# Linear attention on one core: the last pair's Q load cut into unequal software DMAs, the last store in two whole ones

## The chip, the core and the metric

The kernel runs on one core of a Trainium2 chip. The time is device microseconds of one execution, the median of the runs on the chip. An execution with the hardware profiler on gives the page and the trace; its own time stands beside its span below.

## The reference

`Q`, `K` and `V` are float32 arrays of 8 batches, 12 heads, 512 positions and 64 features, 12.58 MB each. Per batch and head:

```python
Q_feat = np.maximum(0, Q) + 1
K_feat = np.maximum(0, K) + 1
KV = np.einsum('bhkd,bhkv->bhdv', K_feat, V)
K_sum = np.sum(K_feat, axis=2)
numerator = np.einsum('bhqd,bhdv->bhqv', Q_feat, KV)
denominator = np.einsum('bhqd,bhd->bhq', Q_feat, K_sum)
return (numerator / (denominator[:, :, :, None] + 1e-10)).astype(np.float32)
```

The output is float32, another 12.58 MB. Every input is read once and the output written once.

## The kernel before, in words

The 96 heads are worked on in twelve groups of eight, two groups to a pair, so there are six pairs (`s` = 0 to 5, groups `2*s` and `2*s + 1`). A pair's load of one input is 2 MB: 128 partitions, and per partition two runs (`n`) of 32 rows of 64 values, 8 KB of float32 each. The loads are issued from GpSimd (POOL) as software DMAs, since they convert float32 to bfloat16 on the way into SBUF; only the very first half of Q comes through SyncE (SP) as float32. `load_pair(s)` issues V, K and Q of a pair in this order (L111, L111, L124). In the first pair each input comes in halves.

For each group VectorE makes the features of K and Q (`feature`, L154), and VectorE and ScalarE together spread V into four masked blocks (`v_blocks`, L171 and L173). TensorE multiplies features of K with the blocks of V (`keys_values`, L195); a column of ones in the blocks gives the sum of K's features in the same product. ScalarE copies the result to SBUF (L209). Q's features are transposed on TensorE (L222) and copied by ScalarE (L227). `out_matmuls` (L237) makes numerators and denominators, and `norms` on VectorE takes the reciprocal (L253) and the product (L254) into `o_sb`, the pair's output tile in SBUF.

The order is written out by hand (`manual_schedule`): `iteration(s)` works on the keys of pair `s` while the outputs of pair `s - 1` are finished; each engine runs its instructions in the order of the program and waits on semaphores. `load_pair(s + 2)` is issued after iteration `s`, and the load of the last pair (s = 5) after iteration 3. The stores of the first six groups are held back until then, so that POOL issues them behind all loads; the stores of groups 6 and 7 follow iteration 4 and those of groups 8 and 9 iteration 5. Each of these ten is one software DMA of 1 MB (L138). The software DMAs take their completion semaphores from a ring of eight, in the order of issue.

The last two groups are stored through SP (hardware DMAs). Group 10 is one DMA of 1 MB (L143). Group 11 is cut: pairs of heads 1 and 5 in one DMA of 512 KB (L146), 3 in one of 256 KB (L147), and 7 in three: the last two of its eight rows per partition (512 bytes) in one DMA of 123 partitions and one of 5 (L150), and the first six rows in one of 128 (L151).

A DMA's data moves through sixteen DMA engines that all queues share. The trace records a completion step of each engine for each DMA, and each packet's queue, start, duration and size, but not the engine that moved it.

Of the kernel before, what the change touches and what calls it, by code (L numbers as in the profile page):

```python
# [19 lines left out]
def kernel(  # L20
# [15 lines left out]
    nc = tc.nc  # L36

    B, H, S, D = Q.shape
    P = 128
    C = 8  # L40
# [4 lines left out]
    NP = 4  # L45
    NG = NPAIR // NP
# [4 lines left out]
    def view(t, c):  # L51
        return t.flatten_outer_dims().rearrange("(n p c) d -> p n c d", p=P, c=c)

    q_eights = view(Q, C4)
# [30 lines left out]
    outs = {}  # L85
# [35 lines left out]

    def load_q(s):
        t = in_pool.tile([P, 2, C4, D], BF16, name="q_raw")
        nc.gpsimd.dma_start(out=t, in_=q_eights[:, 2 * s : 2 * s + 2])  # L124
        rows = t.rearrange("p n (r c) d -> p n r c d", c=C)
        for e in range(2):
            raw["q", 2 * s + e] = [rows[:, n, :, 4 * e : 4 * e + 4] for n in range(2)]

    def load_pair(s):
        load("v", (2 * s, 2 * s + 1))  # L130
        load("k", (2 * s, 2 * s + 1))
        load_q(s)

    def store(g):
        s = g // 2
        o_to = o_dram[:, 2 * NP * s : 2 * NP * s + 2 * NP]
        if g < NG - 2:
            nc.gpsimd.dma_start(  # L138
                out=o_to[:, g % 2 : 2 * NP : 2], in_=outs[s][:, g % 2 : 2 * NP : 2], single_packet=True
            )  # L140
            return
        if g == NG - 2:
            nc.sync.dma_start(out=o_to[:, 0 : 2 * NP : 2], in_=outs[s][:, 0 : 2 * NP : 2])  # L143
            return
        o_sb = outs[s]
        nc.sync.dma_start(out=o_to[:, 1 : 2 * NP : NP], in_=o_sb[:, 1 : 2 * NP : NP])  # L146
        nc.sync.dma_start(out=o_to[:, 3], in_=o_sb[:, 3])  # L147
        cut = C - 2
        for ps in (slice(0, 123), slice(123, P)):
            nc.sync.dma_start(out=o_to[ps, 7, cut:], in_=o_sb[ps, 7, cut:])  # L150
        nc.sync.dma_start(out=o_to[:, 7, 0:cut], in_=o_sb[:, 7, 0:cut])  # L151

    def feature(dst, src):
        nc.vector.tensor_scalar(  # L154
# [167 lines left out]
    with tc.manual_schedule():  # L322
# [8 lines left out]
            out=mask,  # L331
            in_=identity.rearrange("p (h b x) -> p b h x", h=2, b=4),
# [3 lines left out]
        for i in range(2):  # L336
            t = v_all[:, i].rearrange("p n c b x -> p (n c) b x")
            nc.vector.memset(t[:, :, :, D1:], 0.0)
            nc.vector.tensor_copy(  # L339
                out=t[:, :, :, D], in_=mask[:, None, :].to_broadcast([P, 2 * C2, 4])  # L340
# [18 lines left out]
        for s in range(1, NG // 2):  # L359
            iteration(s)  # L360
            if s + 2 < NG // 2:
                load_pair(s + 2)
            for g in range(2 * s - 2, 2 * s) if s > 3 else range(2 * s) if s == 3 else ():
                store(g)
        output(NG - 2)
        output(NG - 1)
        for g in range(NG - 2, NG):
            store(g)
# [30 lines left out]
```

## Time and profile before

| | |
|---|---|
| median of 3 runs | 126.42 us (126.39 to 126.56) |
| profiled execution, its own time | 126.47 us |
| its span, first to last instruction | 124.7 us |
| TensorE busy | 72.2 us (58%) |
| VectorE busy | 81.9 us (66%) |
| ScalarE busy | 68.4 us (55%) |
| GpSimd busy, DMA issues included | 24.8 us (20%) |
| HBM read and written | 37.75 MB and 12.58 MB, 404 GB/s over the span |
| software DMA queue | 7520 packets, 28.84 MB, 93.9% of the DMA engines' time |
| hardware DMA queue | 1368 packets, 3.15 MB, 6.8% |

A load's packets are counted by what they write, which is half of what they read, since the type is halved on the way; a store's packets are counted in full. In the row of slices each digit is a fortieth of the span. "POOLq" and "SPq" are the two issuing queues. The time from a DMA's issue to its landing holds the time that it waited behind other DMAs in the queue.

### The profile page before, as it was taken

To read this page: it belongs to the slowest core of one execution; us is meant where nothing else is said; L and a number is where in the kernel's file an instruction comes from. 1 tells how busy PE (TensorE), PEld (TensorE's weight loads), DVE (VectorE), ACT (ScalarE), POOL (GpSimd) and SP (SyncE) were. 2 spreads that over 40 slices of the span, in tenths; PEclk is the share of its full clock that TensorE was granted. 3 is DMA by queue.
4 is the path that set the end of the run, shared out by engine and by line. 5 is a ranking of instruction groups with operands and counts; after the bars stand their busy time and mean duration, and the time that the engine had idled before them with its cause. 6 is when DMAs were issued, how large, how long until landed. Compare 5 with 4: busy or idle time off the path is not lost.

```text
span 124.7 us, 3086 instructions
## 1 busy us (share of the span) xinstructions
PE 72.2 (58%) x1344; PEld 54.4 (44%) x1344; DVE 81.9 (66%) x185; ACT 68.4 (55%) x73; POOL 24.8 (20%) x52
## 2 busy tenths in 40 slices
PE   0000199692397949976796927979429995550000
PEld 0000299591266725754465714567216774320000
DVE  0475643006679997999979979798997945990000
ACT  0005827928955999199947998059990196000000
POOL 6990001500000600033000890220210202000000
PEclk9999999999859995899769995599975799955555
DMA  3999999999999999999999999999999999999991
GB/s 74 344 216 217 214 212 210 214 214 222 210 212 210 218 222 212 212 212 214 221 214 213 212 216 216 218 213 210 214 350 422 413 417 413 413 413 418 411 388 64
DMA packets 8902, 32.18 MB, mean 258 GB/s; under 512 B 568, under 2 KB 824, under 8 KB 8760
## 3 DMA queue, kind: packets, MB, share of 16 engines
q0 software_dynamic: 7520, 28.84, 93.9%
q1 hardware_dynamic: 1368, 3.15, 6.8%
q8 instruction: 10, 0.16, 0.5%
q14 instruction: 4, 0.03, 0.1%
HBM read 37.75 MB, written 12.58 MB: 404 GB/s over the span
## 4 chain that ended last, share of the span: by engine, by line
PE 32%; DMA 21%; ACT 18%; DVE 14%; issue 3%; POOL 1%; ACTq 0%; POOLq 0%
PE kva_ps L195 21%; DMA k_raw<-in_K_dram 14%; ACT qt L227 9%; PE o_ps L237 7%; DMA v_raw<-in_V_dram 7%; ACT v_all L173 6%; DVE o_sb L254 6%; DVE v_all L171 4%; PE qt_ps L222 4%; ACT kva_all L209 2%; DVE kf L154 2%; DVE recip L253 1%; ACT L173 1%; POOL v_raw L111 1%; POOL k_raw L114 1%
## 5 line engine op out<-in xcount | busy, mean ns | idle before, releaser
L195 PE MATMUL kva_ps<-v_all,kf 64*64 64x272 bf16 x768 | 41.0, 330 | 19.9 <-ACT v_all L173 18.3
L195 PEld LDWEIGHTS <-kf 64*64 64x64 bf16 x768 | 28.3, 125 | 25.7 <-DVE v_all L171 16.4
L173 ACT ACTIVATE v_all<-v_raw,mask 128x1024 bf16<-128x1024 bf16 (+1 forms) x24 | 36.5, 1578 | 3.1 <-DMA v_raw<-in_V_dram 3.0
L254 DVE TENSOR_TENSOR o_sb<-o_ps,recip 128x512 f32<-128x512 f32 x48 | 33.2, 691 | 1.7
L227 ACT COPY qt<-qt_ps 128x1024 bf16<-128x1024 bf16 x24 | 22.7, 1024 | 19.6 <-PE qt_ps L222 19.6
L237 PE MATMUL o_ps<-kva_all,qt 128*64 128x130 bf16 x384 | 21.4, 253 | 14.1 <-ACT kva_all L209 9.2
L237 PEld LDWEIGHTS <-qt 128*64 128x64 bf16 x384 | 14.9, 126 | 23.8 <-issue 9.6
L171 DVE TENSOR_SCALAR v_all<-v_raw,mask 128x2048 bf16<-128x2048 bf16 (+1 forms) x36 | 22.0, 665 | 3.2 <-DMA v_raw<-in_V_dram 3.2
L154 DVE TENSOR_SCALAR kf<-k_raw 128x1024 bf16<-128x1024 bf16 x24 | 9.4, 434 | 12.0 <-DMA k_raw<-in_K_dram 12.0
L222 PE MATMUL qt_ps<-identity,qf 128*128 128x128 bf16 x192 | 13.7, 219 | 4.9 <-ACT qt L227 4.8
L253 DVE RECIPROCAL recip<-o_ps 128x8 f32<-128x8 f32 x48 | 9.6, 201 | 8.3 <-PE o_ps L237 8.2
L111 POOL DMA_DIRECT2D v_raw<-in_V_dram x5 | 3.7, 730 | 53.5 <-ACT qt L227 23.7
L222 PEld LDWEIGHTS <-qf 128*128 128x128 bf16 x192 | 11.2, 97 | 7.0 <-issue 6.4
L138 POOL DMA_DIRECT2D out_dram<-o_sb x10 | 8.1, 819 | 25.5 <-DVE o_sb L254 13.7
L209 ACT CAST kva_all<-kva_ps 64x260 bf16<-64x260 f32 x24 | 9.0, 374 | 3.8 <-PE kva_ps L195 3.5
L154 DVE TENSOR_SCALAR qf<-q_raw 128x1024 bf16<-128x1024 bf16 x22 | 8.2, 430 | 0.1
L173 ACT ACT_TABLE_LOAD x1 | 1.3, 1283 | 10.7 <-DMA v_raw<-in_V_dram 10.7
L124 POOL DMA_DIRECT2D q_raw<-in_Q_dram x5 | 3.6, 722 | 0.0
L111 POOL DMA_DIRECT2D k_raw<-in_K_dram x5 | 3.6, 719 | 0.0
L330 DVE TENSOR_REDUCE mask<-identity 128x4 f32<-128x128 bf16 x1 | 0.3, 285 | 4.7 <-POOL identity masks.py:199 4.7
L344 POOL MEMSET kva_all<- 128x130 bf16 x16 | 2.4, 204 | 0.0
L339 DVE CAST v_all<-mask 128x128 bf16<-128x128 f32 x2 | 2.2, 1644 | 0.0
(11 smaller groups left out, 6.0 us busy)
## 6 DMA issues: line engine op xcount, KB each, us to landing
out_dram<-o_sb POOLq DMA_DIRECT2D x10, 1024.0 KB, 24.6
v_raw<-in_V_dram POOLq DMA_DIRECT2D x5, 1024.0 KB, 13.5
k_raw<-in_K_dram POOLq DMA_DIRECT2D x5, 1024.0 KB, 17.7
q_raw<-in_Q_dram POOLq DMA_DIRECT2D x5, 1024.0 KB, 21.9
o_sb<-in_Q_dram SPq DMA_DIRECT2D x1, 1024.0 KB, 5.0
k_raw<-in_K_dram POOLq DMA_DIRECT2D x2, 512.0 KB, 9.7
v_raw<-in_V_dram POOLq DMA_DIRECT2D x2, 512.0 KB, 11.6
out_dram<-o_sb SPq DMA_DIRECT2D x1, 1024.0 KB, 11.5
```

Of the source, the lines that this page charges most:

```text
L111: nc.gpsimd.dma_start(out=t, in_=drams[x][:, 2 * s : 2 * s + 2])
L138: nc.gpsimd.dma_start(out=o_to[:, g % 2 : 2 * NP : 2], in_=outs[s][:, g % 2 : 2 * NP : 2], single_packet=True)
L154: nc.vector.tensor_scalar(out=dst, in0=src, scalar1=1.0, scalar2=1.0, op0=ALU.add, op1=ALU.max)
L171: nc.vector.tensor_scalar_mul(block[:, 0:cut], v_raw[:, 0:cut], mask[:, b : b + 1])
L173: nc.scalar.mul(out=block[:, cut:], in_=v_raw[:, cut:], mul=mask[:, b : b + 1])
L195: nc.tensor.matmul(halves[h][64 * eight : 64 * eight + 64, 0 : 4 * DV], lhsT=kf[ps, c, n, :], rhs=v_all[ps, g % 2, n, c], start=first, sto ...
L209: nc.scalar.copy(out=kva[ps, :, n, :], in_=halves[h][ps, 0 : 4 * DV].rearrange("p (b x) -> p b x", b=4)[:, :, 0:D1],)
L222: nc.tensor.transpose(qt_ps[g][half][:, c, r], qf[:, r, 2 * half + c, :, :], identity)
L227: nc.scalar.copy(out=qts[g // 2][:, lo : lo + 2], in_=t.rearrange("p c r q -> p c q r"))
L237: nc.tensor.matmul(o_ps[64 * j : 64 * j + 64, c // 2 % 2, (c % 2) * W : (c % 2) * W + W], lhsT=qt[:, c, q : q + 16, :], rhs=kva[:, b], sta ...
L253: nc.vector.reciprocal(out=recip, in_=cells[:, :, :, :, D:D1])
L254: nc.vector.tensor_tensor(out=outs[g // 2][:, 2 * h + g % 2 : 2 * NP : NP, 4 * i : 4 * i + 4].rearrange("p n (b c) d -> p b c n d", b=2), ...
```

## The change

The Q load of the last pair (s = 5) becomes six software DMAs. The first four of the 32 rows, for both runs `n`, are loaded by five DMAs over 51, 4, 51, 5 and 17 partitions, which together are the 128; then the other 28 rows are loaded by one DMA over all 128 partitions. The values and where they are put in `q_raw` stay the same, and so do the other pairs.

The last group's store becomes two hardware DMAs of 512 KB over all 128 partitions: pairs of heads 1 and 5, as before, and 3 and 7.

```diff
     def load_q(s):
         t = in_pool.tile([P, 2, C4, D], BF16, name="q_raw")
-        nc.gpsimd.dma_start(out=t, in_=q_eights[:, 2 * s : 2 * s + 2])
+        q_from = q_eights[:, 2 * s : 2 * s + 2]
+        cut = 0
+        if s == NG // 2 - 1:
+
+            cut = 4
+            lo = 0
+            for n in (51, 4, 51, 5, 17):
+                ps = slice(lo, lo + n)
+                nc.gpsimd.dma_start(out=t[ps, :, 0:cut], in_=q_from[ps, :, 0:cut])
+                lo += n
+        nc.gpsimd.dma_start(out=t[:, :, cut:], in_=q_from[:, :, cut:])
         rows = t.rearrange("p n (r c) d -> p n r c d", c=C)
...
         if g == NG - 2:
             nc.sync.dma_start(out=o_to[:, 0 : 2 * NP : 2], in_=outs[s][:, 0 : 2 * NP : 2])
             return
-        o_sb = outs[s]
-        nc.sync.dma_start(out=o_to[:, 1 : 2 * NP : NP], in_=o_sb[:, 1 : 2 * NP : NP])
-        nc.sync.dma_start(out=o_to[:, 3], in_=o_sb[:, 3])
-        cut = C - 2
-        for ps in (slice(0, 123), slice(123, P)):
-            nc.sync.dma_start(out=o_to[ps, 7, cut:], in_=o_sb[ps, 7, cut:])
-        nc.sync.dma_start(out=o_to[:, 7, 0:cut], in_=o_sb[:, 7, 0:cut])
+        nc.sync.dma_start(out=o_to[:, 1 : 2 * NP : NP], in_=outs[s][:, 1 : 2 * NP : NP])
+        nc.sync.dma_start(out=o_to[:, 3 : 2 * NP : NP], in_=outs[s][:, 3 : 2 * NP : NP])
```

## The prediction

> **What bounds the kernel now.** I read the page first: it has no compute engine above 66%, but the DMA row is full from the second slice on.
>
> ```profile
> PE 72.2 (58%) x1344; PEld 54.4 (44%) x1344; DVE 81.9 (66%) x185; ACT 68.4 (55%) x73; POOL 24.8 (20%) x52
> ...
> DMA  3999999999999999999999999999999999999991
> GB/s 74 344 216 217 214 212 210 214 214 222 210 212 210 218 222 212 212 212 214 221 214 213 212 216 216 218 213 210 214 350 422 413 417 413 413 413 418 411 388 64
> ```
>
> The loads count at half their size here (float32 read, bfloat16 written: 215 GB/s written is 430 read), the stores at full size. So the transfers run at one rate all along, and the end is the end of the DMA queues. The timeline of the last stretch agrees: VectorE's last product ends at 112.05 us, and SyncE has nothing left to issue after 117.9.
>
> ```profile
> 111.36 0.69 DVE L254 TENSOR_TENSOR o_sb<-o_ps,recip 128x512 f32<-128x512 f32 x1
> 112.08 0.34 SPq L147 DMA_DIRECT2D out_dram<-o_sb  x1
> 112.46 4.28 SPq L150 DMA_DIRECT2D out_dram<-o_sb  x2
> 116.78 1.11 SPq L151 DMA_DIRECT2D out_dram<-o_sb  x1
> ```
>
> The table by stretches says how it runs out: full to 121, a third busy after.
>
> ```profile
> 118.00:121.00 3.00, 0.00 (x0) 0.00 (x0) 0.00 (x0) 0.00 (x0) 0.00 (x0) 0.50 1.04 405
> 121.00:124.00 3.00, 0.00 (x0) 0.00 (x0) 0.00 (x0) 0.00 (x0) 0.00 (x0) 0.50 0.34 125
> ```
>
> Who is still busy then? The trace keeps, for each DMA, sixteen completion steps, one per DMA engine, without the engine's name. For the DMA landed at 97.50 us eight engines finish at 96.14 to 96.69 and eight at 97.26 to 97.50. For the one landed at 111.33, seven finish by 109.22, seven by 110.04, two at 111.27 and 111.33. For the very last store, fourteen finish between 121.31 and 122.58 and two at 123.70 and 123.75. So two late engines set the end, 1.1 us behind the next. Their lateness has a visible cause: the page's queues hold instruction loads beside the data.
>
> ```profile
> q8 instruction: 10, 0.16, 0.5%
> q14 instruction: 4, 0.03, 0.1%
> ```
>
> Each of the ten 16 KB packets took 0.89 to 1.03 us of one engine, and after each of them one engine's completions step back by 1.1 to 1.2 us. The first eight hit eight different engines; the ninth (97.41 us) and tenth (105.27) hit two of these again, and these are the two late ones. The 8 KB packets (0.31 us; 44.6, 72.7, 102.3 and 116.65 us) put one or two of the other eight behind as well. When compute ends there are seven leaders and nine laggards, among them the two last.
>
> **What the change moves, part by part.** Prices of packets: hardware stores of 512 B took 27 ns, of 1,536 B 65, of 2,048 B 84, so about 8 ns a packet and 0.037 ns a byte. A 2 MB load occupies each engine 4.89 us (landings 87.55 to 92.45) for 128 KB: 26.8 GB/s.
>
> (1) The last store. Per engine, pairs 3 and 7 are now eight 2,048 B and eight 1,536 B packets: 0.67 + 0.52 = 1.19 us, and three engines also get 41 packets of 512 B (1.1 us). That it is three shows in the trace: the 123-partition store has three completions from data, the 5-partition one five. After it, every engine has sixteen packets of 2,048 B, 1.34 us, and one completion step less: +0.14 us on the two late engines, which is on the path. Three SyncE issues (4.28 + 1.11 us) become less than 0.4 us; they hide behind the queue's backlog now (last issue 117.9, data moving to 123.7), so that is worth nothing.
>
> (2) The main Q load shrinks from 8 KB to 7 KB a row on 16 rows per engine: 16 KB at 26.8 GB/s, -0.61 us on every engine.
>
> (3) The 256 KB taken out come back in pieces of 1 KB read. I take how a count of partitions is dealt out from the stores: 123 went to 3 engines, 5 to 5, 128 to 16, in each the largest divisor up to 16. Then 51 goes to 3 engines (17 partitions each), 4 to 4, 5 to 5, 17 to 1 engine. Together 3 + 4 + 3 + 5 + 1 = 16: if each begins where the last ended, seven engines carry 17 partitions and nine carry 1. No row shows software DMAs of this size, so I bound a 1 KB piece: 38 ns at the bulk rate, 46 by the packet prices. Two pieces a partition: 34 pieces cost 1.29 to 1.56 us, two cost 0.08 to 0.09. Completion steps: 9 ns (hardware) to 22 ns (software median) each, one to five more per engine: 0.01 to 0.11. Net with (2): a light engine gets -0.53 to -0.41, a heavy one +0.69 to +1.06. I take -0.43 and +1.0, near the dear end, since small packets were dear in the store.
>
> The rule for these shares is also in the Trainium skill, "DMA: Bandwidth & Descriptors", section "Why a DMA increments its semaphore by 16 and not by 1": largest common divisor up to 16, software DMAs on consecutive engines from a cursor that goes round. The store's three and five completions agree with the divisor; no run here shows the cursor. The same section notes an exception, software copies dealt out over all sixteen; that is the second rival.
>
> (4) POOL's queue. The five added issues cost some 0.55 to 0.72 us each, and POOL is 80% idle. More matters who they wait for. Software DMAs use eight semaphores in turn, and each waits for the one eight before it. The waits show it, and POOL's timeline its first case: the store at 78.04 came 0.3 us after the Q load of eight DMAs earlier landed (77.76).
>
> ```profile
> POOL out_dram L138 <- DMA v_raw<-in_V_dram: 4.4, 1, 4.4
> ...
> POOL out_dram L138 <- DMA q_raw<-in_Q_dram: 3.2, 1, 3.2
> ```
>
> ```profile
> 70.58 0.72 POOL L124 DMA_DIRECT2D q_raw<-in_Q_dram  x1
> 71.29 3.51 POOL L138 DMA_DIRECT2D out_dram<-o_sb  x4
> 78.04 0.75 POOL L138 DMA_DIRECT2D out_dram<-o_sb  x1 [3.24 <-DMA q_raw<-in_Q_dram]
> 83.22 0.85 POOL L138 DMA_DIRECT2D out_dram<-o_sb  x1 [4.42 <-DMA v_raw<-in_V_dram]
> ```
>
> With five more in the ring, the fifth small load waits for the K load that landed at 72.87, and the main Q load takes the place of the store at 78.04; behind it on POOL stand all ten stores. The first then waits for the V load (82.67), the second for the K load (87.55), the next five only for small loads that have landed, so by 93 us eight stores are issued, as before. Cover: at 78.7 the queue still holds V until 82.67, K until 87.55 and the small pieces; the first store, issued near 83.5, is wanted at about 92. Cost nothing; without that cover each microsecond of an empty queue is a microsecond of time.
>
> (5) Q's landing. Light engines end it near 92.0, heavy ones that lead now (91.1 to 91.6) near 92.6; VectorE reads Q at 96.84. Four microseconds of room, so nothing; nor do the extra semaphore waits on VectorE, which has 8 us of backlog behind it.
>
> **Sum.** If both late engines are light: -0.43 + 0.14 = -0.29 us. The profiled execution took 126.47 with a span of 124.7, 1.8 us around it; the median of the runs is 126.42. 126.42 - 0.29 = 126.13. Next in line: leaders finished pair 3 at 120.65 to 121.15; with a whole pair 7 (0.65) and a heavy share they end by 122.9, before 123.46. A middle engine (pair 3 done by 122.03) with a heavy share ends at 123.4 to 123.7, just level with the late ones. So 126.03 to 126.40 in this case.
>
> Why light? The three engines of the 123-partition store must be leaders: a middle one (121.74) with 1.1 + 0.52 us more would end at 123.4, and none ends between 122.58 and 123.70. The two further engines of the 5-partition store end among the middle ones. So a first heavy block of three and then light ones fits what the store shows, and seven heavy and nine light are the counts of leaders and laggards. That is fit, not proof: the starting engine is unseen.
>
> **Rivals.** *A late engine gets a heavy share* (the slower side). One of the two twice-hit engines lies in a block of 51 or carries the 17. It ends at 123.75 + 0.14 + 1.06 = 124.95, +1.2 us: 127.6; at the cheap end +0.83, 127.25. It decides as soon as one late engine is heavy, since 1.1 us separate them from the rest. Against: the fit above. For: the blocks' start. The Trainium skill (same page, "Latency and other measured facts") says engines 7 and 15 are usually slower. With the blocks counted from 0, 7 opens the second 51 and 15 carries the 17, so by that rule this rival holds; the trace has no pair apart until 97.4 us, only after instruction packets, which speaks against it.
>
> *The shares do not come out as blocks* (the change doesn't do what it says). If all sixteen engines share each small load about evenly, each gets sixteen pieces: -0.61 + 0.74 + 0.11 = +0.24, with the store +0.38: 126.8. If each starts at engine 0 with a sixteenth, rounded up, per engine (4, 1, 4, 1, 2 partitions), engines get 0 to 12 partitions, and a late one with ten pays +0.56: 127.0. For: every software DMA of before ran on sixteen engines. Against: the divisor in the stores.
>
> *Nothing gained*: a middle engine is heavy at the dear price, or the instruction packets fall otherwise once SyncE's issues are gone; 126.4 to 126.6.
>
> **How the numbers follow.** Late engines light 0.56, late engine heavy 0.20, no blocks 0.17, nothing gained 0.07. A difference under 0.2% (0.25 us) is about what a measurement of this kernel can't tell from none; the forecast's -0.29 lies just beyond it, so of its 0.56 I count 0.42 as faster and 0.14 as same. Same: 0.14 + 0.04 = 0.18. Slower: 0.20 + 0.17 + 0.03 = 0.40. Range: from 125.95, the forecast's cheap end of 126.03 less the 0.08 us that runs differ by, through no blocks to the lower part of the heavy case, 127.4. The forecast's own range is 126.0 to 126.4.
>
> **What would show it.** Page: more software packets of 512 B, fewer hardware packets, no L150. Completions: small loads with heavy engines late; the last store's two latest near 123.45 and the heavy leaders near 122.8. POOL: main Q issue near 78, first store near 83. Wrong if the last completions are near 125 (heavy late engine), if all engines shift alike (no blocks), or if the DMA row shows a gap between 78 and 95 (the semaphore ring).

## The result, and the profile after

The kernel with the change takes 126.68 us (median, 126.55 to 126.87) against 126.42 before in the same runs; the ratio is 1.0020, with a 95% interval of 1.0014 to 1.0027. So it is 0.26 us slower, where 0.29 us less was forecast. The profiled execution took 126.70 us with a span of 124.9.

The page's DMA rows of the changed kernel, to be held against those of before: the row stays at 9, that is 90% or more, and two slices near the place of the cut Q load (the 28th and 30th, 181 and 321 GB/s) move less than before (210 and 350). The page's queue rows stand below, the software queue's of before last.

```profile
DMA  3999999999999999999999999999999999999992
GB/s 94 331 211 214 218 214 214 211 215 216 216 211 212 216 215 215 211 212 222 211 215 211 216 218 214 211 214 181 212 321 418 412 417 415 413 412 416 416 409 84
...
q0 software_dynamic: 9296, 28.84, 94.7%
q1 hardware_dynamic: 1216, 3.15, 6.6%
```

```profile
q0 software_dynamic: 7520, 28.84, 93.9%
```

The software queue has 1,776 packets more for the same 28.84 MB. 256 are the small pieces of Q and 80 the completion steps of five more DMAs; the other 1,440 are packets of 4 bytes that nothing in the program asks for, 9 ns each in their records. They are called fillers below.

The end, in the table by stretches: the last three microseconds are half full instead of a third, so more is still being moved when the late engines finish.

```profile
118.00:121.00 3.00, 0.00 (x0) 0.00 (x0) 0.00 (x0) 0.00 (x0) 0.00 (x0) 0.50 1.03 407
121.00:124.00 3.00, 0.00 (x0) 0.00 (x0) 0.00 (x0) 0.00 (x0) 0.00 (x0) 0.50 0.50 195
```

The completion steps of the last store lie at 122.35 to 122.86 for twelve engines, then 123.12, 123.67, 123.98 and 124.01. Before, the last two were 123.70 and 123.75.

POOL's timeline shows the ring of eight semaphores as forecast: the main Q load (L134) waits for the Q load that landed at 77.61, the first store for V, the second for K, and from the second on six go out in a row.

```profile
70.51 4.24 POOL L132 DMA_DIRECT2D q_raw<-in_Q_dram  x5
77.89 0.74 POOL L134 DMA_DIRECT2D q_raw<-in_Q_dram  x1 [3.14 <-DMA q_raw<-in_Q_dram]
82.85 0.80 POOL L148 DMA_DIRECT2D out_dram<-o_sb  x1 [4.22 <-DMA v_raw<-in_V_dram]
87.74 5.22 POOL L148 DMA_DIRECT2D out_dram<-o_sb  x6 [4.09 <-DMA k_raw<-in_K_dram]
```

SyncE has three issues left at the end, done by 112.4.

```profile
108.62 0.39 SPq L153 DMA_DIRECT2D out_dram<-o_sb  x1
110.30 0.37 SPq L155 DMA_DIRECT2D out_dram<-o_sb  x1
111.98 0.37 SPq L156 DMA_DIRECT2D out_dram<-o_sb  x1
```

### The profile page after: what moved, and what is told of

Its sections match the earlier page's. It is cut to its first block, busy times and chain, and to the rows that moved or that the text cites. A ratio compares the mean times of both kernels' runs of the same rounds, so it can differ in the third digit from the quotient of the medians.

```text
span 124.9 us, 3090 instructions
## 1 busy us (share of the span) xinstructions
PE 70.5 (56%) x1344; PEld 53.2 (43%) x1344; DVE 82.5 (66%) x185; ACT 68.3 (55%) x73; POOL 29.2 (23%) x57
## 3 DMA queue, kind: packets, MB, share of 16 engines
q0 software_dynamic: 9296, 28.84, 94.7%
## 4 chain that ended last, share of the span: by engine, by line
DMA 34%; PE 21%; DVE 18%; ACT 13%; issue 2%; POOL 2%; ACTq 0%; POOLq 0%
DMA k_raw<-in_K_dram 27%; PE kva_ps L200 15%; DMA v_raw<-in_V_dram 7%; DVE o_sb L259 6%; DVE v_all L176 6%; ACT qt L232 5%; ACT v_all L178 5%; PE o_ps L242 4%; DVE kf L159 2%; PE qt_ps L227 2%; DVE qf L159 2%; DVE recip L258 1%; ACT kva_all L214 1%; POOL v_raw L111 1%; ACT L178 1%
## 5 line engine op out<-in xcount | busy, mean ns | idle before, releaser
L200 PE MATMUL kva_ps<-v_all,kf 64*64 64x272 bf16 x768 | 39.5, 322 | 20.9 <-ACT v_all L178 18.1
L200 PEld LDWEIGHTS <-kf 64*64 64x64 bf16 x768 | 27.6, 122 | 26.1 <-DVE v_all L176 18.0
L242 PE MATMUL o_ps<-kva_all,qt 128*64 128x130 bf16 x384 | 20.9, 249 | 14.6 <-ACT kva_all L214 8.9
L176 DVE TENSOR_SCALAR v_all<-v_raw,mask 128x2048 bf16<-128x2048 bf16 (+1 forms) x36 | 22.6, 685 | 3.1 <-DMA v_raw<-in_V_dram 3.1
L134 POOL DMA_DIRECT2D q_raw<-in_Q_dram x5 | 3.7, 733 | 3.1 <-DMA q_raw<-in_Q_dram 3.1
L132 POOL DMA_DIRECT2D q_raw<-in_Q_dram x5 | 4.2, 866 | 0.0
```

Of the source, the lines that this page charges most:

```text
L176: nc.vector.tensor_scalar_mul(block[:, 0:cut], v_raw[:, 0:cut], mask[:, b : b + 1])
L200: nc.tensor.matmul(halves[h][64 * eight : 64 * eight + 64, 0 : 4 * DV], lhsT=kf[ps, c, n, :], rhs=v_all[ps, g % 2, n, c], start=first, sto ...
L242: nc.tensor.matmul(o_ps[64 * j : 64 * j + 64, c // 2 % 2, (c % 2) * W : (c % 2) * W + W], lhsT=qt[:, c, q : q + 16, :], rhs=kva[:, b], sta ...
```

## The experiments

All ratios are to the kernel before, in runs on the same chip; a diff is against it unless the text names another kernel. "Two whole stores" means the change's last store.

### The two halves apart

e1 has the change's store alone:

```diff
...
-        nc.sync.dma_start(out=o_to[:, 3], in_=o_sb[:, 3])
-        ...
-        nc.sync.dma_start(out=o_to[:, 7, 0:cut], in_=o_sb[:, 7, 0:cut])
+        nc.sync.dma_start(out=o_to[:, 3 : 2 * NP : NP], in_=outs[s][:, 3 : 2 * NP : NP])
```

e2 has the change's Q load alone:

```diff
+        ...
+            for n in (51, 4, 51, 5, 17):
+                ps = slice(lo, lo + n)
+                nc.gpsimd.dma_start(out=t[ps, :, 0:cut], in_=q_from[ps, :, 0:cut])
+                lo += n
+        nc.gpsimd.dma_start(out=t[:, :, cut:], in_=q_from[:, :, cut:])
```

> Q is loaded in one DMA as before; only the last store is changed to two DMAs of 512 KB. All theories: each late engine moves sixteen packets of 2,048 B (1.34 us) for eight of 2,048 and eight of 1,536 (1.19 us), so +0.14 us: 126.56. If it gives 0 or less, the three-way cut of the last store was worth nothing and the whole +0.26 us of the change comes from the Q load.

> Q cut into the six DMAs, the store left as before. Empty-step theory (each software DMA over fewer than sixteen engines costs every engine some 18 extra 4-byte steps, about 0.19 us): light engines get 5 x 0.19 + 0.1 for their own pieces - 0.61 for the smaller main load, that is some +0.15 less what overlaps, so +0.1 to +0.2 us: about 126.55. Rival (light engines do gain 0.43 us, and a heavy engine that an instruction load also hits sets the end): the light late engines are at 123.3, the end is set by the heavy engine, which no longer has the larger store behind it: 0 to -0.1 us, about 126.35.

e1: 126.53 us, ratio 1.0009 (1.0000 to 1.0017), so +0.1 us as expected. e2: 126.61 us, ratio 1.0014 (1.0006 to 1.0023), so +0.18. The halves add up to the whole. The Q cut, which was to bring 0.43, costs. In e2's trace the three engines of the 123-partition store finish it at 122.85, 123.17 and 123.34 instead of 121.59, 121.90 and 122.07: these three carry a heavy share, 1.27 us later. The blocks are there.

### What a piece costs, and what a small DMA costs

e3 is e2 with one size:

```diff
-            for n in (51, 4, 51, 5, 17):
+            for n in (128,):
```

e4 leaves Q whole and adds, ahead of it in the last pair:

```diff
+            ...
+            for n in (3, 4, 3, 3, 3):
+                ps = slice(lo, lo + n)
+                nc.gpsimd.dma_start(out=spare[ps], in_=q_eights[ps, 2 * s, 0:4])
+                lo += n
         nc.gpsimd.dma_start(out=t, in_=q_eights[:, 2 * s : 2 * s + 2])
```

> The same four rows in ONE software DMA over all 128 partitions, store as before: sixteen pieces of 1 KB on each engine, no block, no DMA on fewer than sixteen engines. This prices the pieces: at 60 ns a piece 0.96 - 0.61 + 0.02 = +0.37 us (126.8); at 42 ns, if the pieces overlap as the large packets do, +0.08 (126.5). The empty-step theory expects 16 extra 4-byte packets in the whole run; the rival has no opinion on that.

> Q whole, store as before, and five spare software DMAs of 3, 4, 3, 3 and 3 partitions ahead of the last Q load, one piece of 1 KB per partition into a tile that nobody reads: one piece for each engine in all, so no engine is loaded more than another. Empty-step theory: 5 x 0.19 + 0.06 = +1.0 us (127.4) and some 1,500 more 4-byte software packets. Rival (only bytes and shares cost): one piece and five steps, +0.1 to +0.15 us (126.55), and 80 more 4-byte packets.

e3: 126.53 us, ratio 1.0007 (0.9998 to 1.0015). In its trace the Q load takes the earliest engine from 86.18 to 91.11, 4.93 us, where 4.89 was usual: sixteen pieces cost 0.65 us for the 0.61 saved, 41 ns each, inside the forecast's 38 to 46 although each packet's record lasts 60 ns. e4: 126.46 us, ratio 1.0007 (0.9998 to 1.0016). Five small DMAs as such cost next to nothing; the theory of a fixed price for each, which I had taken from the 0.18 us between their completion steps, is wrong. The page's queue row of e4 says why the number of 4-byte packets matters:

```profile
q0 software_dynamic: 7680, 28.85, 94.0%
```

160 packets more than before: 16 pieces, 80 steps and 64 fillers, one for each engine that a DMA left out (13 + 12 + 13 + 13 + 13). In the change it is not one but one for every piece of a loaded engine: 13 x 34 + 12 x 2 + 13 x 34 + 11 x 2 + 15 x 34 = 1,440, exactly the count. That gives the next theory: fillers cost by their number.

### The fillers alone

```diff
+            ...
+            for n in (51, 4, 51, 5, 17):
+                ps = slice(lo, lo + n)
+                nc.gpsimd.dma_start(out=spare[ps], in_=q_eights[ps, 2 * s : 2 * s + 2, 0:1])
+                lo += n
         nc.gpsimd.dma_start(out=t, in_=q_eights[:, 2 * s : 2 * s + 2])
```

> Q whole, store as before, and ahead of the last Q load five spare software DMAs of the change's sizes, one row of each of the two runs (256 B read) into a tile that nobody reads: hardly any bytes, but the shape of the change. Filler theory (a DMA with two runs per partition is dealt out in blocks, and every engine left out takes one 4-byte packet per piece of the loaded ones): 1,520 more 4-byte packets, +0.66 us and two small pieces on each light engine, the late ones among them: 127.1 to 127.2. Rival (fillers are hidden, as the five small DMAs of e4 were): 126.5 to 126.6.

That is e12: 127.07 us against 126.38, ratio 1.0053 (1.0039 to 1.0066): +0.67 us for pieces of 256 bytes and their fillers. The queue row has as many packets as the change's:

```profile
q0 software_dynamic: 9296, 28.88, 94.5%
```

A late engine, if no block holds it, takes 34 + 34 + 34 + 2 = 104 of them, so about 6 ns each, and the two last steps of the last store come at 124.32 and 124.37, 0.62 later than before. The 6 ns are an estimate: they put all of the 0.67 us down to the fillers of a light engine. By the count such an engine gets nothing else but two pieces and five steps, and e4 shows that steps cost next to nothing; no run changes the number of fillers alone.

### Eight rows of one run

```diff
+            cut = 8
+            ...
+            for n in (51, 4, 51, 5, 17):
+                ps = slice(lo, lo + n)
+                nc.gpsimd.dma_start(out=t[ps, 0, 0:cut], in_=q_from[ps, 0, 0:cut])
+                lo += n
+            nc.gpsimd.dma_start(out=t[:, 0, cut:], in_=q_from[:, 0, cut:])
+            nc.gpsimd.dma_start(out=t[:, 1], in_=q_from[:, 1])
```

That is e5, with two whole stores. e6 and e7 have twelve rows and other sizes, to move the second heavy block:

```diff
-            cut = 8
-            for n in (51, 4, 51, 5, 17):
+            cut = 12
+            for n in (51, 5, 34, 5, 17, 16):     # e6
+            for n in (51, 4, 34, 6, 17, 16):     # e7
```

> The last store in two DMAs; the same five sizes and the same bytes, but as eight rows of the first run instead of four rows of both: half as many pieces, each of 2 KB read; the rest of Q in two DMAs of 128 partitions. Filler theory (each engine that a small software DMA leaves out takes one 4-byte packet for every piece of a loaded engine, about 6.3 ns each): 720 fillers instead of 1,440, so a light engine gets -0.61 + 0.08 + 0.33 = -0.20 us for the Q load, a heavy one -0.61 + 17 x 0.079 + 0.23 = +0.96; with the store the late engines stand at about -0.1 us against before, and the heavy engine that an instruction load had hit ends level with them: about 126.35, which is 0.3 us less than the change. Rival (a fixed cost per small DMA): no less than the change, 126.7.

> As e5, with twelve rows of the first run, and the sizes 51, 5, 34, 5, 17 and 16: if the engines are counted from 0, the second heavy block is engines 8 and 9 in place of 7 to 9, and 16 partitions lie evenly on all. Light: -0.92 + 2 x 0.117 + 0.35 = -0.34; heavy: -0.92 + 18 x 0.117 + 0.25 = +1.43. Filler theory with the late heavy engine being number 7: no heavy engine has been hit by an instruction load, late engines at -0.34 + 0.14 = -0.2: about 126.2. With the late heavy engine being 8 or 9: it ends near 123.9 in its trace, +0.15: 126.6.

> As e6 with the sizes 51, 4, 34, 6, 17 and 16, so that the second heavy block is engines 7 and 8. Late heavy engine being number 9: about 126.2; being 7 or 8: about 126.6. Exactly one of e6 and e7 should be the faster, or neither if it is number 8.

e5: 126.05 us, ratio 0.9969 (0.9957 to 0.9981): the same bytes by the same five sizes are now 0.39 us faster than before and 0.6 faster than the change. The expected number of fillers was wrong, though. The queue row

```profile
q0 software_dynamic: 7808, 28.84, 94.4%
```

holds 288 more than before: 128 pieces, 96 steps, and 64 fillers, not 720. And no three engines jump ahead of the rest in the completions of the first 51-partition DMA: each rank rises by about 0.3 us, four pieces. So these DMAs were not dealt out in blocks of 17. A count that fits is a sixteenth of the partitions, rounded up, for each engine, with fillers up to that: 64 - 51 = 13, 16 - 4 = 12, 13, 11 and 32 - 17 = 15. Dealt out from the first engine on, that is 12 partitions on the first four engines and none on the last three.

e6 and e7 missed everything: 129.35 and 128.78 us, ratios 1.0229 (1.0206 to 1.0252) and 1.0186 (1.0167 to 1.0205). Not the shares, but the ring of eight did it. One small DMA more, and the last part of Q waits for the K load that lands at 87.37. POOL's timeline of e6:

```profile
77.86 0.51 POOL L130 DMA_DIRECT2D q_raw<-in_Q_dram  x1 [4.29 <-DMA q_raw<-in_Q_dram]
82.77 0.56 POOL L132 DMA_DIRECT2D q_raw<-in_Q_dram  x1 [4.41 <-DMA v_raw<-in_V_dram]
87.65 0.62 POOL L133 DMA_DIRECT2D q_raw<-in_Q_dram  x1 [4.33 <-DMA k_raw<-in_K_dram]
```

The part before it is done on the first engine at 88.05, and the queue runs short: the stretch from 88 to 92 us of e6 moves 148 GB/s, where the four microseconds ahead of it moved 205. The row of before for the same stretch comes last; its 240 GB/s hold some stores, which are counted in full.

```profile
84.00:88.00 4.00, 2.24 (x64) 1.68 (x56) 2.20 (x6) 3.95 (x6) 0.35 (x1) 1.00 1.08 205
88.00:92.00 4.00, 1.10 (x16) 0.53 (x16) 4.00 (x8) 3.10 (x3) 3.90 (x6) 0.79 0.99 148
```

```profile
88.00:92.00 4.00, 1.40 (x32) 0.95 (x31) 4.00 (x9) 3.93 (x7) 0.75 (x1) 0.96 1.04 240
```

The DMA share is lowest from 89 to 90 us, at 0.79 with 101 GB/s. Around it the packets fill the time but are slow: those of 4,096 bytes that start between 88.3 and 92.5 us last 0.44 us (median), where 0.32 is usual. Why they are slow isn't shown.

So e6 and e7 say nothing on the blocks, and show the price of the cover that the prediction had named for POOL's queue.

### Are the shares the gain?

Three edits of e5; e11 is e10 with the last store of before.

```diff
-            for n in (51, 4, 51, 5, 17):
+            for n in (128,):                     # e9
-            cut = 8
+            cut = 12                             # e10, e11
```

> Control for e5, which came out 0.39 us faster than before: the same eight rows of the first run and the same two DMAs for the rest, but the eight rows in one DMA of 128 partitions, so that every engine has eight pieces. Theory of shares (in e5 the small DMAs were dealt out from the first engine on, a sixteenth of the partitions rounded up to each: 12 partitions on the first four engines, none on the last three, and the late engines are among the light ones): the gain is gone, the pieces cost 8 x 0.079 - 0.61 = +0.02 and the store +0.1: 126.5. Rival (the gain comes from the Q load being two large DMAs, or from where the stores come to lie): as e5, 126.05.

> e5 with twelve rows in place of eight. Theory of shares: an engine with no partition gets -0.92 in place of -0.61, one with twelve +0.48 in place of +0.34; the late engines end 0.3 us earlier, the middle ones with many partitions now set the end near 123.0 in the trace: 125.8 to 125.95. Rival (gain not from the shares): as e5, 126.05, or a little dearer.

> e10 with the last store cut as before. Theory of shares: another -0.1 us on the late engines, unless the first three engines, which now carry 12 partitions of Q as well as the 123-partition store (1.1 us), set the end: 122.6 + 0.48 = 123.1: 125.75 to 125.95. If the two cuts load the same engines so much that these become the last, slower than e10.

e9: 126.88 us, ratio 1.0037 (1.0024 to 1.0051). Without unequal shares the gain is gone. It is even 0.35 us above its own sum. Its trace shows where that may come from: 26 of the 128 pieces of its first Q DMA last 132 to 301 ns in place of 98, together 2.3 us more. That is enough to hold up seven engines by 0.3 us each, and the last seven steps of the Q load come at 92.50 to 93.10 us, where the last eight of before came at 92.19 to 92.45. In e5's trace no such piece lasts over 98 ns. Which engines had the slow pieces, and why they are slow, stays open; without the 0.35 us e9 would still be 0.5 us slower than e5. e10: 125.84 us, ratio 0.9962 (0.9947 to 0.9977); e11: 125.97, ratio 0.9966 (0.9954 to 0.9979). More rows help as expected; the old store, which was to bring another 0.1 us, adds nothing to it. In e11's trace the engine that finishes first ends at 120.42, where the first of before ended at 121.31: 0.89 us less, about what an engine without any of the twelve rows saves (0.92). And as far as the ranks of the steps tell, the two engines that the ninth and tenth 16 KB instruction loads hit were ahead of most others before the hit (96.41 us in a DMA that reaches 97.78 for the one, 103.94 in one that reaches 105.32 for the other; these places are empty in the next DMA): the late engines are among the light ones.

### Which rule deals out

e13 has the change's pieces, but both from one run; e14 and e15 are e10 with other sizes.

```diff
+            to = t[:, 0].rearrange("p (a b) d -> p a b d", b=16)     # e13
+            ...
+                nc.gpsimd.dma_start(out=to[ps, :, 0:4], in_=fr[ps, :, 0:4])
-            for n in (51, 4, 51, 5, 17):
+            for n in (52, 52, 24):                                   # e14
+            for n in (104, 24):                                      # e15
```

> The change's five sizes and its 1 KB pieces, two per partition, but both from the first run (rows 0 to 3 and 16 to 19), the rest of Q in two DMAs of 128, the last store in two. If what makes a small DMA go out in blocks with fillers is that it has more than one piece per partition, then 1,440 fillers as in the change, and the light late engines get +0.13 us and the store's +0.1: 126.65 (about 2,016 4-byte software packets). If it is that the DMA spans both runs, or the size of the pieces, then 64 fillers, 12 partitions on the first engines and none on the last three: -0.61 on the late ones, as e5: 126.05, 640 packets of 4 bytes.

> Twelve rows of the first run as in e10, but by three DMAs of 52, 52 and 24 partitions. Rule of dealing out (a one-run DMA starts at the first engine and gives each a sixteenth of its partitions, rounded up): 4 + 4 + 2 = 10 partitions on engines 0 to 11, 8 on the thirteenth, none on the last three. Late engines, if among these: -0.92, and the others only +0.25 where e10 gave up to +0.48, so the middle engines no longer set the end: 122.8 in the trace, about 125.6 to 125.8, not slower than e10. If the shares start elsewhere for each DMA (a cursor), all engines come out nearly even: 126.5 or more, as e9.

> The same twelve rows by two DMAs of 104 and 24 partitions. Same rule: 7 + 2 = 9 partitions on engines 0 to 11, 7 on the two after them, 6 on the fifteenth and none on the last alone. If the late engines are the two before the last (the traces of e10 and e11 have one leader and two others that come out light), they get only -0.92 + 7 x 0.117 = -0.10 and the gain is nearly gone: 126.4 to 126.5. If one of them is the last engine, that one is relieved and the other still sets the end: the same time. Only if both gains came from few and large pieces would it be as fast as e14.

e13: 126.73 us, ratio 1.0021 (1.0012 to 1.0029), the change's loss again, and its queue row

```profile
q0 software_dynamic: 9440, 28.84, 94.9%
```

has 1,920 packets more than before: 256 pieces, 128 more packets for the rest of the run, which now comes in two parts, 96 steps and 1,440 fillers. So, of what these runs tell apart, it is the two pieces per partition that make a small DMA go out in blocks with a filler for every piece.

e14: 125.75 us, ratio 0.9941 (0.9927 to 0.9954), e15: 126.63, ratio 1.0012 (1.0003 to 1.0020). The rule from the first engine on forecast both, e14 to the tenth, e15 0.1 to 0.2 us too low. They have the same rows and the same kind of DMAs, and differ in who gets them: in e14 three engines get none, in e15 one. In e14 the two last steps of the last store are 123.03 and 123.06, with ten of the sixteen engines within 0.6 us; in e15 they are 123.78 and 123.98, 1.1 us behind the next. Since two engines still trail in e15, neither of them is the one that it leaves out: by the rule's count the late two are the two before the last. The stretches of e14 at the end:

```profile
118.00:121.00 3.00, 0.00 (x0) 0.00 (x0) 0.00 (x0) 0.00 (x0) 0.00 (x0) 0.50 1.02 398
121.00:124.00 3.00, 0.00 (x0) 0.00 (x0) 0.00 (x0) 0.00 (x0) 0.00 (x0) 0.50 0.34 130
```

The last stretch of e14 is busy for a third of its time, as before (0.34, 125 GB/s), but over by 123.1; the table doesn't tell the two apart, the completion steps do. e14 beats both kernels, by 0.7 us the one before and, by the two ratios, by 1.0 the change.

### More of the last store on the first three engines

```diff
-        cut = C - 2
+        cut = C - 4
```

> Q whole; the last store cut as before, but four of pair 7's eight rows go to the DMAs of 123 and 5 partitions instead of two, so the three engines of the 123 get 41 packets of 1 KB (about 46 ns each, 1.9 us) and the late engines eight packets of 1 KB instead of 1.5 KB: -0.15 us on the late engines. The three leaders end at 121.1 + 1.9 + 0.37 = 123.4 or earlier, below the late ones at 123.6. Expected 126.3. If shares do not matter: 126.45.

e8: 126.31 us, ratio 0.9990 (0.9981 to 0.9999): about 0.1 us, as expected and as small. It agrees with the price of the store term in the other direction, as far as so small a difference can.

## Why the prediction was wrong, point by point

*What bounds the kernel* held. The end is the end of two DMA engines that the instruction loads had put behind: e14 takes work from three engines, by the rule the late two among them, and gives it to the others; the time falls by 0.7 us while the compute engines run the same instructions. One reading is off: the ninth and tenth instruction load set their engine back by 1.4 to 1.5 us, not by 1.1 to 1.2 as the ones before them did (before: 101.25, where its place in the order had been about 99.9, and 108.84, where it had been about 107.35). The sum doesn't use it.

*(1) The last store*, +0.14: measured +0.1 (e1, 0.0 to 0.2 by its interval). Right.

*(2) and (3), the pieces*: 41 ns for a 1 KB piece, inside the 38 to 46. Blocks of 17 and 1 came out as the divisor of the stores had suggested: the filler count is that of blocks on 3, 4, 3, 5 and 1 engines, and e2's store steps show that the three engines of the 123-partition store are heavy. The Trainium skill ("DMA: Bandwidth & Descriptors", section "Why a DMA increments its semaphore by 16 and not by 1") has this rule, and beside it the exception with a sixteenth rounded up. The runs agree with both, each in its place: two pieces per partition go by the first (the change, e12, e13), one piece per partition by the second (e5, e10, e14).

*The term that failed* is the last of (3): "Completion steps: 9 ns (hardware) to 22 ns (software median) each, one to five more per engine: 0.01 to 0.11." A light engine took not five extra 4-byte packets but, by the count of fillers, over a hundred more, since every DMA fills the engines it leaves out with as many packets as the loaded ones have pieces. e12 puts that at 0.67 us, two tiny pieces included. With the 0.09 for its own two pieces it gives 0.67 + 0.09 - 0.61 = +0.15 us for a light engine in place of -0.43; e2 measured +0.18. The sum is then 0.15 + 0.1 = +0.25, and the change measured +0.26. The heavy share was too small for the same reason: +0.69 to +1.06 forecast, 1.27 measured in e2, which 34 x 0.041 - 0.61 plus 72 fillers at 6 ns gives as 1.2. I had bounded the cost of steps by rows of whole DMAs over sixteen engines, and no row of before had a software DMA on fewer; the bound from above should have allowed for something per piece.

*(4) POOL's queue* held: main Q issued at 77.89, first store at 82.85, the eighth store at 94.06, a microsecond later than forecast. The cover was real, and e6 shows what its loss costs: 2.9 us. *(5) Q's landing* held too: its last step is at 93.52, and VectorE reads Q from 97.2 on.

*The rivals.* The heavy late engine did not set this end by a full share: 124.95 was its price, and the last steps are at 124.01. One heavy engine was a middle one, so the seven heavy engines are not the seven leaders: the Q load's last step is at 93.52, 0.8 us after the next. Followed from DMA to DMA it ends at 123.67, 0.3 us before the light late ones, near the 123.4 to 123.7 of "next in line", and doesn't set the end. Whether engines 7 and 15 are slow of themselves can't be read from traces that name no engine; the pair that ends last is the pair that instruction loads hit twice, and by the rule's count in e14 and e15, from 0, it is engines 13 and 14. "No blocks" is what one-run DMAs do, not these. "Nothing gained", the rival at 126.4 to 126.6, came nearest in size, by a mechanism that it did not name. The range held the result only because it was stretched for rivals that did not happen. That is luck; the sign was wrong.

## What to carry to other kernels

Where the DMA queues are the end, ask which engine ends last and by how much; the completion steps of the last DMA tell. Here work could be taken from it by the sizes of small software DMAs with one contiguous piece per partition; with two, each engine left out paid about 6 ns for every piece of a loaded one, which ate up the gain. And a software DMA added is a place taken in the ring of completion semaphores: count who waits for whom eight DMAs later.

## What the runs showed of the hardware that I had not expected

- Software DMAs that leave out engines send them 4-byte packets: one per piece of a loaded engine with two pieces per partition (1,440 in the change), up to the rounded share with one (64 in e5, 32 by the rule in e14, whose queue row has 224 more packets: 128 pieces, 64 steps, 32 fillers). One count fits both: each of the sixteen engines is filled up to the number of pieces of the most loaded one. They last 9 ns in the record and, by the estimate from e12, cost about 6.
- The completion steps of DMAs that follow each other at once are about 0.18 us apart even where they move nothing (e4), and that spacing is hidden: it is no price.
- A 1 KB piece whose packet lasts 60 ns in the record takes 41 ns of its engine in a full queue (e3).
- Open: e9 and e15, with nearly even shares, are 0.35 and 0.1 to 0.2 us above their sums. In e9 slow pieces of the first Q DMA may account for it, without a cause for them; e15's trace shows no such pieces.
